# Linear attention on one core: K and V loaded in rows of 8 KB, V's blocks made by masks, the first matmul in 64x64 tiles

## The chip, the cores and the metric

The kernel runs on one core of one Trainium2 chip. The metric is the device time of one execution in microseconds (us), the median of several runs. A profile is taken of one execution; its span runs from the first instruction to the last, and the time measured for a run is a little longer than such a span.

## The reference

Q, K and V are float32 arrays of shape (8, 12, 512, 64): 96 heads, each with 512 rows of 64 numbers.

```
Q_feat = np.maximum(0, Q) + 1
K_feat = np.maximum(0, K) + 1
KV = np.einsum('bhkd,bhkv->bhdv', K_feat, V)
K_sum = np.sum(K_feat, axis=2)
numerator = np.einsum('bhqd,bhdv->bhqv', Q_feat, KV)
denominator = np.einsum('bhqd,bhd->bhq', Q_feat, K_sum)
return numerator / (denominator[:, :, :, None] + 1e-10)
```

Each head needs a 64x64 matrix KV and a vector K_sum of 64 sums, and then every row of Q is multiplied by both.

## The kernel before

**Groups and layout.** The 96 heads are cut into 12 groups of eight heads (NG = 12), and two groups make a pair, so there are six pairs. In SBUF a partition holds whole rows of the sequence. Q is read in "eights": 128 partitions, each with C4 = 32 rows, which is 8 KB of float32 per partition and covers eight heads. K and V are read in "fours": each partition holds C2 = 16 rows, 4 KB of float32, which covers four heads, so that partitions 32b to 32b+31 belong to head b of four. A group is two such fours of K and V.

**Loads.** GpSimd (POOL) issues nearly all transfers, because they cast float32 to bf16 on the way. `load` (line 105) makes a load of K or V: for the first pair one of 512 KB (bf16) per group, later one of 1 MB per pair, which is 2 MB in HBM. `load_q` (line 119) does the same for Q. `load_pair(s)` (line 126) issues K, V and Q of pair s in this order, and each of these three names has two buffers, so the loads of pair s+2 wait on POOL until the groups of pair s have used theirs up. The first Q alone goes over SP's queue and lands as float32 in an output tile (line 93).

**Work on a group g.** `k_features` (line 155) computes max(K + 1, 1) on VectorE (DVE) in two instructions. `v_blocks` (line 162) copies V into v_all: a zeroed buffer in which each partition has four blocks of 64 columns, one for each head of the four, and four more columns with ones; only the block of the partition's own head is filled, so the buffer is a block diagonal. Three of the four copies run on DVE (line 169), the fourth on ScalarE (ACT, line 167); each works on 32 partitions and 2048 elements. `keys_values` (line 180) multiplies: for 16 positions c and two fours n, the 128x64 features are the stationary operand and 260 columns of v_all the moving one, summed in PSUM; n picks the half of PSUM's partitions, and so the column half of TensorE (PE). Block b of the result is KV of head b of the four, and the last four columns are the sums. Four copies on ACT (lines 195 and 196) then bring it into kva, a block-diagonal buffer for two heads. `transposes` (line 198) turns Q's features over (PE, then a copy on ACT, line 209), `out_matmuls` (line 211) multiplies them by kva in 16 matmuls for each half of a pair's heads (h), and `norms` (line 228) divides on DVE: a reciprocal (line 236) and a product (line 237) for each of two PSUM tiles. `output(g)` does this for h = 0 and 1. It needs kva of both groups of its pair. `store` (line 131) issues the result.

**Order.** The order is written by hand and every engine follows it in order. In round g of the loop (line 280) come: the transposes of g-1 if g is odd, k_features(g), v_blocks(g), output(g-2), then either Q's features for the pair (g even) or the transposes of g (g odd), and keys_values(g). At the end of an odd round the loads of a later pair are issued. The stores of groups 0 to 4 are issued in round 7, behind the last loads on POOL's queue; the stores of groups 10 and 11 go over SP's queue, group 11's in five pieces (lines 143 to 148). The last two groups have an order of their own (lines 300 to 315).

**Start.** `clear` (line 251) zeroes a buffer of v_all with a memset on DVE and a copy on ACT, and copies the ones. The identity for the transposes and the zeros of kva are made on POOL.

Of the kernel before, what the change touches and what calls it, by code (L numbers as in the profile page):

```python
# [8 lines left out]
FP32 = mybir.dt.float32  # L9
BF16 = mybir.dt.bfloat16  # L10
ALU = mybir.AluOpType

BANK = 512
# [6 lines left out]
def kernel(  # L20
# [12 lines left out]

    nc = tc.nc  # L40

    B, H, S, D = Q.shape
    P = 128
    C = 8
    C2 = 2 * C
    C4 = 4 * C
# [3 lines left out]
    NG = NPAIR // NP  # L50
    D1 = D + 1
    W = 2 * D1

    def view(t, c):
        return t.flatten_outer_dims().rearrange("(n p c) d -> p n c d", p=P, c=c)

    q_eights = view(Q, C4)
    k_dram = view(K, C2)
    v_dram = view(V, C2)
    o_dram = view(out, C)  # L60

    const = ctx.enter_context(tc.tile_pool(name="const", bufs=1))
    in_pool = ctx.enter_context(tc.tile_pool(name="in_pool", bufs=IN_BUFS))
# [5 lines left out]
    psum_kva = ctx.enter_context(tc.tile_pool(name="psum_kva", bufs=2, space=bass.MemoryType.PSUM))  # L69
# [2 lines left out]

    identity = const.tile([P, P], BF16, name="identity")
    NV = 4
    v_all = const.tile([P, 2, 2, C2, 4 * D1], BF16, name="v_all")
    ones = const.tile([P, 4], BF16, name="ones")
    zero = const.tile([P, 1], FP32, name="zero")
    kva_all = const.tile([P, NV, 4, 2, D1], BF16, name="kva_all")
    kva_diag = [kva_all[:, i] for i in range(NV)]

    drams = dict(k=k_dram, v=v_dram)
    raw = {}
    bufs = {}
# [2 lines left out]
    qts = {}  # L86
    outs = {}
    cells_of = {}

    def load_first_q():  # L90
        t = out_pool.tile([P, 2 * NP, C, D], FP32, name="o_sb")
        half = t[:, 0:NP].rearrange("p n c d -> p (n c) d")
        nc.sync.dma_start(out=half, in_=q_eights[:, 0])
        return half

    def load_rest_q(t):
        u = in_pool.tile([P, 2, C4, D], BF16, name="q_raw")
        nc.gpsimd.dma_start(out=u[:, 1], in_=q_eights[:, 1])
        for e in range(2):
            raw["q", e] = [  # L100
                x.rearrange("p (r c) d -> p r c d", c=C)[:, :, 4 * e : 4 * e + 4]
                for x in (t, u[:, 1])
            ]

    def load(x, groups):
        s = groups[0] // 2
        if groups[0] % 2 == 0 or (x, s) not in bufs:
            bufs[x, s] = in_pool.tile([P, 4, C2, D], BF16, name=f"{x}_raw")
        if len(groups) == 2:
            ms = slice(0, 4)  # L110
            of = slice(4 * s, 4 * s + 4)
        else:
            ms = slice(groups[0] % 2, 4, 2)
            of = slice(4 * s + groups[0] % 2, 4 * s + 4, 2)
        nc.gpsimd.dma_start(out=bufs[x, s][:, ms], in_=drams[x][:, of])  # L115
        for g in groups:
            raw[x, g] = bufs[x, s][:, g % 2 : 4 : 2]

    def load_q(s):
        t = in_pool.tile([P, 2, C4, D], BF16, name="q_raw")  # L120
# [5 lines left out]
    def load_pair(s):  # L126
        load("k", (2 * s, 2 * s + 1))
        load("v", (2 * s, 2 * s + 1))
        load_q(s)
# [25 lines left out]
    def k_features(g):  # L155
        k_raw = raw.pop(("k", g))
        kf = kf_pool.tile([P, C2, 2, D], BF16, name="kf")
        for n in range(2):
            feature(kf[:, :, n], k_raw[:, n])
        kfs[g] = kf  # L160

    def v_blocks(g):
        v_raw = raw.pop(("v", g))
        for b in range(4):
            ps = slice(32 * b, 32 * b + 32)
            if b == 3:
                nc.scalar.copy(out=v_all[ps, g % 2, :, :, b * D : b * D + D], in_=v_raw[ps])  # L167
            else:
                nc.vector.tensor_copy(  # L169
                    out=v_all[ps, g % 2, :, :, b * D : b * D + D], in_=v_raw[ps]  # L170
                )

    def q_features(g):
        q_raw = raw.pop(("q", g))
# [4 lines left out]

    def keys_values(g):  # L180
        kf = kfs.pop(g)
        kva_ps = psum_kva.tile([P, 4 * D1], FP32, name="kva_ps")
        for c in range(C2):
            for n in range(2):
                nc.tensor.matmul(  # L185
                    kva_ps[64 * n : 64 * n + 64],
                    lhsT=kf[:, c, n, :],
                    rhs=v_all[:, g % 2, n, c, :],
                    start=(c == 0),
                    stop=(c == C2 - 1),  # L190
                )
        kva = kva_diag[g % NV]
        for n in range(2):
            ps = slice(64 * n, 64 * n + 64)
            nc.scalar.copy(out=kva[ps, :, n, 0:D], in_=kva_ps[ps, 0 : 4 * D].rearrange("p (b d) -> p b d", b=4))  # L195
            nc.scalar.copy(out=kva[ps, :, n, D], in_=kva_ps[ps, 4 * D : 4 * D1])  # L196

    def transposes(g):
        qf = qfs.pop(g)
        if g % 2 == 0:  # L200
            qts[g // 2] = mid_pool.tile([P, C, P, R], BF16, name="qt")
        for half in range(2):
            qt_ps = psum_qt.tile([P, 2, R, P], BF16, name="qt_ps")
            for c in range(2):
                for r in range(R):
                    nc.tensor.transpose(qt_ps[:, c, r], qf[:, r, 2 * half + c, :, :], identity)  # L206
            copy = nc.vector.tensor_copy if half and g == NG - 2 else nc.scalar.copy
            lo = g % 2 * 4 + 2 * half
            copy(out=qts[g // 2][:, lo : lo + 2], in_=qt_ps.rearrange("p c r q -> p c q r"))  # L209

    def out_matmuls(g, h):
# [3 lines left out]
        for c in range(C):  # L215
            for j in range(2):
                b = 2 * (g % 2) + j
                q = 16 * (4 * h + b)
                nc.tensor.matmul(  # L219
                    ops[c // 4][64 * j : 64 * j + 64, c // 2 % 2, (c % 2) * W : (c % 2) * W + W],  # L220
                    lhsT=qt[:, c, q : q + 16, :],
# [6 lines left out]
    def norms(g, h):  # L228
# [17 lines left out]
    def output(g):  # L246
        for h in range(2):
            out_matmuls(g, h)
            norms(g, h)

    def clear(i):
        t = v_all[:, i].rearrange("p n c x -> p (n c x)").bitcast(FP32)
        w = t.shape[1] * 5 // 8
        nc.vector.memset(t[:, 0:w], 0.0)  # L254
        nc.scalar.copy(out=t[:, w:], in_=zero.to_broadcast([P, t.shape[1] - w]))  # L255
        nc.vector.tensor_copy(
            out=v_all[:, i, :, :, 4 * D : 4 * D1].rearrange("p n c j -> p (n c) j"),
            in_=ones[:, None, :].to_broadcast([P, 2 * C2, 4]),
        )

    with tc.manual_schedule():
        nc.gpsimd.memset(zero, 0.0)
        q_first = load_first_q()
        load("k", (0,))
        load("v", (0,))
        load_rest_q(q_first)
        load("k", (1,))
        load("v", (1,))
        nc.vector.memset(ones, 0.0)
        for b in range(4):  # L270
            nc.vector.memset(ones[32 * b : 32 * b + 32, b : b + 1], 1.0)
        clear(0)
        make_identity(nc, identity)
        for t in kva_diag:
            for b in range(4):
                nc.gpsimd.memset(t[:, b], 0.0)  # L276
        load_pair(1)
        clear(1)
        last = NG - 1
        for g in range(last - 1):  # L280
            if g % 2:
                transposes(g - 1)
            k_features(g)
            v_blocks(g)
            if g >= 2:
                output(g - 2)
            if g % 2:
                transposes(g)
            else:
                q_features(g)  # L290
# [59 lines left out]
```

## Time and profile before

| what | value |
|---|---|
| device time, median of 3 runs | 126.78 us (126.35 to 127.07) |
| span of the profiled execution, the only time it has | 124.5 us |
| last o_sb computed / last store landed | 111.25 us / 123.56 us |
| busy PE, DVE, ACT, POOL | 52%, 72%, 48%, 21% of the span |
| HBM read / written | 37.75 MB / 12.58 MB |
| TensorE clock granted, mean | 0.816 |

In the rows of the profile L185 and the like are lines of the kernel above; times in a timeline count from the span's start. In a row of a group the shape stands as partitions x elements, then the count. The row of slices cuts the span into 40 parts of 3.1 us, each digit the busy share in tenths. PE's row of matmuls and PEld's row of weight loads overlap. A transfer has an issue, on POOL or SP, and lands later; a row of DMA shares above 1.00 means that packets overlap on the 16 engines.

### The profile page before, as it was taken

The page shows a single profiled execution, that of the slowest core. Times are in us where ns is not written, and L with a number is a line of the kernel's source. Part 1 is how long each engine was busy: PE and PEld are TensorE (multiplying, and loading weights), DVE is VectorE, ACT ScalarE, POOL GpSimd, SP SyncE. Part 2 cuts the span into 40 slices and gives each one's busy share as a digit, 9 for nine tenths or more (in the row PEclk, how much of TensorE's full clock was granted, in tenths as well). Part 3 has the DMA queues.
Part 4 walks back from the last instruction along what each step waited for, and adds up shares of the span by engine and source line. Part 5 has one row for each costly group of instructions (what it writes and reads, how often), then busy time and mean ns, then how long its engine had stood idle before and what let it go on. Part 6 is the DMA issues. An engine that isn't in the chain of part 4 may idle for free.

```text
span 124.5 us, 2350 instructions
## 1 busy us (share of the span) xinstructions
PE 65.0 (52%) x960; PEld 53.1 (43%) x960; DVE 89.7 (72%) x190; ACT 59.6 (48%) x86; POOL 26.6 (21%) x53
## 2 busy tenths in 40 slices
PE   0000874600596837939197495987756987420000
PEld 0000754600475736829175374866635766210000
DVE  4875744206999989997999989999599996970000
ACT  7505069706009981398807767169990355000000
POOL 6992020400001310204002194202203302000000
PEclk9999999985559996799859959689985599955555
DMA  3999999999999999999999999999999999999993
GB/s 95 319 211 218 204 209 212 209 215 218 207 212 212 220 215 205 212 213 216 212 213 211 213 219 211 213 209 216 214 295 421 420 419 411 416 414 416 417 407 140
DMA packets 11971, 32.13 MB, mean 258 GB/s; under 512 B 568, under 2 KB 824, under 8 KB 11832
## 3 DMA queue, kind: packets, MB, share of 16 engines
q0 software_dynamic: 10592, 28.84, 97.5%
q1 hardware_dynamic: 1368, 3.15, 6.7%
q8 instruction: 7, 0.11, 0.3%
q14 instruction: 4, 0.03, 0.1%
HBM read 37.75 MB, written 12.58 MB: 404 GB/s over the span
## 4 chain that ended last, share of the span: by engine, by line
DMA 30%; DVE 27%; PE 14%; ACT 10%; POOL 6%; issue 3%; DVEq 0%; ACTq 0%; POOLq 0%
DMA v_raw<-in_V_dram 30%; DVE o_sb L237 12%; PE kva_ps L185 12%; DVE v_all L169 8%; ACT v_all L167 5%; ACT qt L209 3%; DVE recip L236 3%; DVE qf L151 2%; POOL kva_all L276 2%; POOL k_raw L115 2%; ACT kva_all L195 2%; PE qt_ps L206 1%; PE o_ps L219 1%; DVE kf L151 1%; POOL v_raw L115 1%
## 5 line engine op out<-in xcount | busy, mean ns | idle before, releaser
L185 PE MATMUL kva_ps<-v_all,kf 128*64 128x260 bf16 x384 | 34.2, 351 | 15.8 <-DVE v_all L169 14.2
L185 PEld LDWEIGHTS <-kf 128*64 128x64 bf16 x384 | 27.8, 144 | 19.7 <-DVE v_all L169 14.7
L237 DVE TENSOR_TENSOR o_sb<-o_ps,recip 128x512 f32<-128x512 f32 x48 | 33.2, 692 | 1.7
L219 PE MATMUL o_ps<-kva_all,qt 128*64 128x130 bf16 x384 | 19.6, 236 | 28.1 <-DVE recip L236 19.1
L169 DVE COPY v_all<-v_raw 32x2048 bf16<-32x2048 bf16 x36 | 25.5, 710 | 10.5 <-DMA v_raw<-in_V_dram 10.1
L219 PEld LDWEIGHTS <-qt 128*64 128x64 bf16 x384 | 13.7, 116 | 33.1 <-issue 16.9
L167 ACT COPY v_all<-v_raw 32x2048 bf16<-32x2048 bf16 x12 | 22.6, 1894 | 10.8 <-DMA v_raw<-in_V_dram 10.6
L195 ACT CAST kva_all<-kva_ps 64x256 bf16<-64x256 f32 x24 | 8.9, 370 | 31.4 <-PE kva_ps L185 31.2
L209 ACT COPY qt<-qt_ps 128x1024 bf16<-128x1024 bf16 x23 | 22.2, 1015 | 2.5 <-PE qt_ps L206 2.2
L206 PE MATMUL qt_ps<-identity,qf 128*128 128x128 bf16 x192 | 14.1, 229 | 1.3 <-ACT qt L209 1.1
L135 POOL DMA_DIRECT2D out_dram<-o_sb x10 | 8.8, 879 | 23.1 <-DMA q_raw<-in_Q_dram 6.7
L206 PEld LDWEIGHTS <-qf 128*128 128x128 bf16 x192 | 11.8, 103 | 4.1 <-issue 2.2
L115 POOL DMA_DIRECT2D k_raw<-in_K_dram x7 | 5.4, 772 | 37.5 <-DVE kf L151 37.0
L151 DVE TENSOR_SCALAR kf<-k_raw 128x1024 bf16<-128x1024 bf16 x24 | 9.9, 453 | 4.3 <-DMA k_raw<-in_K_dram 4.2
L236 DVE RECIPROCAL recip<-o_ps 128x8 f32<-128x8 f32 x48 | 9.6, 200 | 2.9 <-PE o_ps L219 2.6
L115 POOL DMA_DIRECT2D v_raw<-in_V_dram x7 | 5.4, 768 | 16.5 <-ACT v_all L167 16.5
L151 DVE TENSOR_SCALAR qf<-q_raw 128x1024 bf16<-128x1024 bf16 x22 | 8.1, 424 | 0.0
L254 DVE MEMSET v_all<- 128x2600 f32 x2 | 4.5, 2225 | 1.1 <-issue 1.1
L196 ACT CAST kva_all<-kva_ps 64x4 bf16<-64x4 f32 x24 | 4.1, 169 | 0.0
L121 POOL DMA_DIRECT2D q_raw<-in_Q_dram x5 | 3.5, 704 | 0.0
L255 ACT COPY v_all<-zero 128x1560 f32<-128x1560 f32 x2 | 2.9, 1488 | 0.0
L276 POOL MEMSET kva_all<- 128x130 bf16 x16 | 2.4, 196 | 0.0
(14 smaller groups left out, 6.6 us busy)
## 6 DMA issues: line engine op xcount, KB each, us to landing
out_dram<-o_sb POOLq DMA_DIRECT2D x10, 1024.0 KB, 24.0
k_raw<-in_K_dram POOLq DMA_DIRECT2D x5, 1024.0 KB, 16.7
v_raw<-in_V_dram POOLq DMA_DIRECT2D x5, 1024.0 KB, 17.3
q_raw<-in_Q_dram POOLq DMA_DIRECT2D x5, 1024.0 KB, 21.5
o_sb<-in_Q_dram SPq DMA_DIRECT2D x1, 1024.0 KB, 4.8
k_raw<-in_K_dram POOLq DMA_DIRECT2D x2, 512.0 KB, 9.5
v_raw<-in_V_dram POOLq DMA_DIRECT2D x2, 512.0 KB, 11.3
out_dram<-o_sb SPq DMA_DIRECT2D x1, 1024.0 KB, 12.1
```

Source lines behind the costliest of these rows:

```text
L115: nc.gpsimd.dma_start(out=bufs[x, s][:, ms], in_=drams[x][:, of])
L135: nc.gpsimd.dma_start(out=o_to[:, g % 2 : 2 * NP : 2], in_=outs[s][:, g % 2 : 2 * NP : 2], single_packet=True)
L151: nc.vector.tensor_scalar(out=dst, in0=src, scalar1=1.0, scalar2=1.0, op0=ALU.add, op1=ALU.max)
L167: nc.scalar.copy(out=v_all[ps, g % 2, :, :, b * D : b * D + D], in_=v_raw[ps])
L169: nc.vector.tensor_copy(out=v_all[ps, g % 2, :, :, b * D : b * D + D], in_=v_raw[ps])
L185: nc.tensor.matmul(kva_ps[64 * n : 64 * n + 64], lhsT=kf[:, c, n, :], rhs=v_all[:, g % 2, n, c, :], start=(c == 0), stop=(c == C2 - 1),)
L195: nc.scalar.copy(out=kva[ps, :, n, 0:D], in_=kva_ps[ps, 0 : 4 * D].rearrange("p (b d) -> p b d", b=4))
L206: nc.tensor.transpose(qt_ps[:, c, r], qf[:, r, 2 * half + c, :, :], identity)
L209: copy(out=qts[g // 2][:, lo : lo + 2], in_=qt_ps.rearrange("p c r q -> p c q r"))
L219: nc.tensor.matmul(ops[c // 4][64 * j : 64 * j + 64, c // 2 % 2, (c % 2) * W : (c % 2) * W + W], lhsT=qt[:, c, q : q + 16, :], rhs=kva[:, ...
L236: nc.vector.reciprocal(out=recip, in_=cells[:, :, :, :, D:D1])
L237: nc.vector.tensor_tensor(out=o_sb[:, 2 * h + g % 2 : 2 * NP : NP, 4 * i : 4 * i + 4].rearrange("p n (b c) d -> p b c n d", b=2), in0=cell ...
```

## The change

The fours of K and V become eights, as Q already has them: each partition reads 32 rows, 8 KB of float32 in one piece, and 16 partitions belong to a head. The transfers keep their sizes. In the first pair each group is one eight; later a pair's two eights come in one transfer and a group is one half of the rows (positions) of both eights. So KV of a head is summed over both groups of a pair, and in the first pair over one.

A partition's head is now one of eight: 64 partitions hold four heads, and the two partition halves h hold different heads. `keys_values` therefore multiplies each half by itself: 64 partitions by 64 columns of features, 64 matmuls per group instead of 32, into two PSUM tiles (one for each h), and the copies to kva come once per pair, four of 64x(4x65).

v_all gets four blocks of 68 columns, each with V's 64, a sum column and three of zeros. A mask with one column for each b (made from the identity by a reduction) replaces the copies: each block is V times the mask's column on all 128 partitions. DVE does blocks 0 and 1 and half of block 2, ACT the rest (one instruction of 1024 elements, one of 2048). Nothing has to be cleared but the three zero columns. The line numbers of the functions behind the change shift.

```diff
+    DV = D + 4
-    k_dram = view(K, C2)
-    v_dram = view(V, C2)
+    k_dram = view(K, C4)
+    v_dram = view(V, C4)
...
-    v_all = const.tile([P, 2, 2, C2, 4 * D1], BF16, name="v_all")
-    ones = const.tile([P, 4], BF16, name="ones")
-    zero = const.tile([P, 1], FP32, name="zero")
+    v_all = const.tile([P, 2, 2, C2, 4, DV], BF16, name="v_all")
+    mask = const.tile([P, 4], FP32, name="mask")
...
     def load(x, groups):
         s = groups[0] // 2
-        if groups[0] % 2 == 0 or (x, s) not in bufs:
-            bufs[x, s] = in_pool.tile([P, 4, C2, D], BF16, name=f"{x}_raw")
+        if groups[0] % 2 == 0:
+            bufs[x, s] = in_pool.tile([P, 2, C4, D], BF16, name=f"{x}_raw")
+        t = bufs[x, s]
         if len(groups) == 2:
-            ms = slice(0, 4)
-            of = slice(4 * s, 4 * s + 4)
+            nc.gpsimd.dma_start(out=t, in_=drams[x][:, 2 * s : 2 * s + 2])
         else:
-            ms = slice(groups[0] % 2, 4, 2)
-            of = slice(4 * s + groups[0] % 2, 4 * s + 4, 2)
-        nc.gpsimd.dma_start(out=bufs[x, s][:, ms], in_=drams[x][:, of])
+            n = groups[0] % 2
+            nc.gpsimd.dma_start(out=t[:, n], in_=drams[x][:, 2 * s + n])
         for g in groups:
-            raw[x, g] = bufs[x, s][:, g % 2 : 4 : 2]
+            e = g % 2
+            if s == 0:
+                raw[x, g] = t[:, e].rearrange("p (n c) d -> p n c d", n=2)
+            else:
+                raw[x, g] = t[:, :, C2 * e : C2 * e + C2]
...
     def v_blocks(g):
         v_raw = raw.pop(("v", g))
         for b in range(4):
-            ps = slice(32 * b, 32 * b + 32)
-            if b == 3:
-                nc.scalar.copy(out=v_all[ps, g % 2, :, :, b * D : b * D + D], in_=v_raw[ps])
-            else:
-                nc.vector.tensor_copy(
-                    out=v_all[ps, g % 2, :, :, b * D : b * D + D], in_=v_raw[ps]
-                )
+            block = v_all[:, g % 2, :, :, b, 0:D]
+            cut = 2 if b < 2 else 1 if b == 2 else 0
+            if cut > 0:
+                nc.vector.tensor_scalar_mul(block[:, 0:cut], v_raw[:, 0:cut], mask[:, b : b + 1])
+            if cut < 2:
+                nc.scalar.mul(out=block[:, cut:], in_=v_raw[:, cut:], mul=mask[:, b : b + 1])
...
     def keys_values(g):
         kf = kfs.pop(g)
-        kva_ps = psum_kva.tile([P, 4 * D1], FP32, name="kva_ps")
+        if g % 2 == 0:
+            kva_ps[g // 2] = [psum_kva.tile([P, BANK], FP32, name="kva_ps") for _ in range(2)]
+        halves = kva_ps[g // 2]
         for c in range(C2):
             for n in range(2):
-                nc.tensor.matmul(
-                    kva_ps[64 * n : 64 * n + 64],
-                    lhsT=kf[:, c, n, :],
-                    rhs=v_all[:, g % 2, n, c, :],
-                    start=(c == 0),
-                    stop=(c == C2 - 1),
-                )
-        kva = kva_diag[g % NV]
-        for n in range(2):
-            ps = slice(64 * n, 64 * n + 64)
-            nc.scalar.copy(out=kva[ps, :, n, 0:D], in_=kva_ps[ps, 0 : 4 * D].rearrange("p (b d) -> p b d", b=4))
-            nc.scalar.copy(out=kva[ps, :, n, D], in_=kva_ps[ps, 4 * D : 4 * D1])
+                if g < 2:
+                    eight, first, last_c = g, (c, n) == (0, 0), (c, n) == (C2 - 1, 1)
+                else:
+                    eight, first, last_c = n, g % 2 == 0 and c == 0, g % 2 == 1 and c == C2 - 1
+                for h in range(2):
+                    ps = slice(64 * h, 64 * h + 64)
+                    nc.tensor.matmul(
+                        halves[h][64 * eight : 64 * eight + 64, 0 : 4 * DV],
+                        lhsT=kf[ps, c, n, :],
+                        rhs=v_all[ps, g % 2, n, c],
+                        start=first,
+                        stop=last_c,
+                    )
+        if g % 2 == 0:
+            return
+        for h in range(2):
+            kva = kva_diag[(g - 1 + h) % NV]
+            for n in range(2):
+                ps = slice(64 * n, 64 * n + 64)
+                nc.scalar.copy(
+                    out=kva[ps, :, n, :],
+                    in_=halves[h][ps, 0 : 4 * DV].rearrange("p (b x) -> p b x", b=4)[:, :, 0:D1],
+                )
...
-    def clear(i):
...
+        nc.vector.tensor_reduce(
+            out=mask,
+            in_=identity.rearrange("p (h b x) -> p b h x", h=2, b=4),
+            op=ALU.add,
+            axis=mybir.AxisListType.XY,
+        )
+        for i in range(2):
+            t = v_all[:, i].rearrange("p n c b x -> p (n c) b x")
+            nc.vector.memset(t[:, :, :, D1:], 0.0)
+            nc.vector.tensor_copy(
+                out=t[:, :, :, D], in_=mask[:, None, :].to_broadcast([P, 2 * C2, 4])
+            )
```

More of the change, by code (lines that the diff above doesn't have):

```diff
@@ L88 @@
     cells_of = {}
+    kva_ps = {}
     def load_first_q():
@@ L249, in output @@
             norms(g, h)
-    def clear(i):
[L252 to L258, printed above, removed]
-        )
     with tc.manual_schedule():
-        nc.gpsimd.memset(zero, 0.0)
         q_first = load_first_q()
@@ L268 @@
         load("v", (1,))
[L269 to L272, printed above, removed]
         make_identity(nc, identity)
+        nc.vector.tensor_reduce(
[10 more added lines that the diff above has]
+            )
         for t in kva_diag:
@@ L277 @@
         load_pair(1)
-        clear(1)
         last = NG - 1
```

## The prediction

> **What bounds the kernel now.** I read the slices first, then the queues, then the stretches between landings, then the timelines of ACT and PE for one pair of groups. The slices and the queue, from the page:
>
> ```profile
> DMA  3999999999999999999999999999999999999993
> GB/s 95 319 211 218 204 209 212 209 215 218 207 212 212 220 215 205 212 213 216 212 213 211 213 219 211 213 209 216 214 295 421 420 419 411 416 414 416 417 407 140
> q0 software_dynamic: 10592, 28.84, 97.5%
> ```
>
> From the second slice to the last but one the 16 DMA engines are never idle. Loads count here by their bf16 bytes (212 GB/s written is 424 GB/s read); after 93 us the stores run at 416 GB/s. So the **transfers set the end**: the last o_sb is computed at 111.25, but the last store lands at 123.56 and the span ends at 124.5. Compute may slip until it stands where the transfers end; how far that is, is the question of this change.
>
> The trace marks each landing. Those of pair 1 to 5 follow each other at 4.90, 4.89, 4.94, 4.90, 4.90 us for Q and at 4.95, 4.97, 4.94, 5.01, 5.04, 4.82, 5.00, 4.93 us for K and V, all of 2 MB in HBM. Q has 8 KB rows, K and V have 4 KB rows. The same as stretches, K and V first, then Q (us, busy time of PE, PEld, DVE, ACT, POOL, granted clock, DMA share, GB/s):
>
> ```profile
> 33.97:43.89 9.92, 8.38 (x124) 6.89 (x120) 9.25 (x22) 6.46 (x9) 2.25 (x3) 0.82 1.13 215
> 43.89:48.78 4.89, 2.20 (x46) 1.82 (x44) 4.67 (x10) 2.95 (x6) 0.03 (x1) 0.91 1.05 208
> ```
>
> The longer rows carry no visible advantage in GB/s (the rate counts packets of the neighbouring transfer too); by landings it is 4.906 against 4.958 us. A pair takes 14.75 us of transfers: that is the pace.
>
> ACT over one pair (start, length, line), then PE:
>
> ```profile
> 45.30 1.89 ACT L167 COPY v_all<-v_raw 32x2048 bf16<-32x2048 bf16 x1
> 51.73 0.36 ACT L195 CAST kva_all<-kva_ps 64x256 bf16<-64x256 f32 x1 [4.53 <-PE kva_ps L185]
> 52.65 1.93 ACT L209 COPY qt<-qt_ps 128x1024 bf16<-128x1024 bf16 x2
> 54.60 1.90 ACT L167 COPY v_all<-v_raw 32x2048 bf16<-32x2048 bf16 x1
> 56.60 1.93 ACT L209 COPY qt<-qt_ps 128x1024 bf16<-128x1024 bf16 x2
> 58.96 0.36 ACT L195 CAST kva_all<-kva_ps 64x256 bf16<-64x256 f32 x1 [0.43 <-PE kva_ps L185]
> 59.88 1.89 ACT L167 COPY v_all<-v_raw 32x2048 bf16<-32x2048 bf16 x1
> ```
>
> ```profile
> 48.28 3.40 PE L185 MATMUL kva_ps<-v_all,kf 128*64 128x260 bf16 x32
> 51.62 1.07 PE L206 MATMUL qt_ps<-identity,qf 128*128 128x128 bf16 x16
> 54.85 0.42 PE L219 MATMUL o_ps<-kva_all,qt 128*64 128x130 bf16 x8 [1.59 <-DVE recip L236]
> 56.94 1.98 PE L185 MATMUL kva_ps<-v_all,kf 128*64 128x260 bf16 x32
> ```
>
> These form a **loop** ACT - PE - ACT - PE - ACT: V's blocks of the even group, its keys-values matmuls, its transposes and their copies, V's blocks of the odd group, its matmuls, its casts, and only then, in ACT's order, the next even blocks. Before: 1.9 + 3.4 to 3.7 + 1.08 (four casts) + 1.93 + 1.9 + 2.0 + 1.08 + some 0.35 of hand-overs = 13.8 us. It stands under the pace of 14.75, and ACT's 4.53 us of waiting show the room. DVE needs, per pair, 2x0.75 (kf) + 2x2.05 (L169) + 8x0.845 (L236 with L237) + 1.42 (qf) = 13.8 us, also under it.
>
> **The change, part by part.**
>
> *Rows of 8 KB.* Bytes, number and order of transfers stay; K and V go from 4.958 to Q's 4.906 us. Ten full transfers and four halves: 12 x 0.052 = **-0.6 us**, and only if transfers still set the end. Bounds: 0 (first K, V and Q of 512 KB land 2.48 us apart alike) and -0.7. POOL's issues shorten from 0.77 to Q's 0.70; POOL mostly waits, so this is worth nothing. The Trainium skill (Perfetto Trace Analysis, section DMA Optimizations) says that batching into 4 or 8 KB "can dramatically improve throughput"; by that rule this part would be the gain. The landings above speak against it, since rows of both lengths run side by side here and differ by 1%.
>
> *Start.* Two memsets of 2.23 us and two ACT copies of 1.49 us go; a small reduction behind the identity (POOL, ready near 5.4), two short memsets and copies come. All of it ends near 7.5, before the first K (8.18): nothing. If that cover failed, the first features would start at most 1 us later. But ACT's table load (1.28 us, before at 0.73, long ahead of any data) now stands, in the built order, behind the wait for the first V: V lands at 10.66, the load ends at 12.0.
>
> *V's blocks.* DVE: two products over 2048 and one over 1024 elements for three copies of 2048. By the rows of like shape (copy 0.684, kf 0.42) 1.8 for 2.05 us per group. No row shows a product with a value per partition; bounds are 1.8 and, at the fp32 rows' pace (0.688 per 1024), 3.15. I take 1.8: kf is the same operation with constants. ACT: one over 1024 and one over 2048 for one of 2048. Copy rows give 1.015 + 1.894 = 2.9; I take **3.0**, because the extra operand is in no row; bounds 2.8 and 4.0 (every fixed part twice). The Trainium skill (ScalarE: Activation LUTs, section What ACT_TABLE_LOAD costs) puts 93 ns on each pointer operand: by it 3.1, and the sum 1.2 us later.
>
> *First matmul.* 64 matmuls of 272 columns on four 64x64 tiles for 32 of 260 on two. The row gives a tile one matmul per 0.217 us at half clock (16 in 3.47) and 0.124 at full. If four tiles run side by side: 16 x 0.227 = 3.7 (half clock) or 16 x 0.130 = 2.1, with a tail 2.2 us. If only two do: 7.3 and 4.15. Rows show two column tiles side by side, never two row tiles; I take four, because L219's matmuls follow each other every 0.04 us, so issue leaves room, and keep both ends. In the first pair all of one group goes to one column half, so two tiles work: 32 per tile, half of it before the clock rises, 5.7 us; the second group 4.2.
>
> *Casts.* Eight per pair (4x0.37 and 4x0.17, overlapped: 2.16) become four of 260 columns at 0.37: 1.5, but all after the odd group, so kva of the even group is also late. PSUM for it is one set per pair; it is free, since casts stand ahead of the next even blocks on ACT. Queued behind them: those blocks, and POOL's next V load, which waits for ACT. That load has some 10 us of room (issued 71.1, K ahead of it lands 83.4), of which 6 go.
>
> **The sum.** First pair: 12.0 + 3.0 + 5.7 + 2.5 (transposes 0.55, copies 1.93) + 3.0 + 4.2 + 1.5 + hand-overs = 32.0, where V of pair 1 landed at 29.07; ACT is now late. Loop: 3.0 + 3.7 + 2.5 + 3.0 + 2.2 + 1.5 + 0.35 = **16.25 us**, over the pace. Four of them: casts of group 9 end at 97.0 (before 89.6). From there, as DVE's order is written: four norms of group 8 to 100.9, V blocks and kf of 10 and 11 to 105.3, Q features 106.7, norms of group 9 with its copy 111.3, transposes and matmuls of 11 (start 109.7) 113.0, casts 114.5, eight norms with their start 121.6. Then SP issues the last stores, 0.34 + 0.88 + 0.4 + 0.62 (the store of 5 rows took 4.16 with a full queue ahead; I take the others' 0.4), about 2 us to land (SP's first Q took 4.8, of which 2.5 go to its 1 MB), 0.9 from the last landing to the end of the span: 5.2 in all. Span **126.8** against 124.5. The median shown (126.78) lies 2.3 above the span; so **129.1 us**, 1.8% slower.
>
> **Rivals.**
> 1. *The loop fits* (not slower). If the even matmuls run at full clock (2.2 for 3.7) or ACT is nearer 2.7, the loop is 14.75 to 15.5 and compute ends by 118.7, the point from which the transfers (124.5 - 0.6 = 123.9) set the end again: 126.2 us. For it: the odd matmuls already run at full clock, and L169 gets shorter. Against: PEclk falls to 5 whenever PE is mostly idle, and the even matmuls, at 33.6, 48.3 and 78.4, ran at half; after the change PE waits longer ahead of them. Chance 0.30.
> 2. *Half clock throughout, or tiles that do not overlap by rows*. Odd at half clock too (it was in group 7: 3.42 us): loop 17.75, compute end 129, 136.5 us. No overlap: 5.7 + 4.15 in the loop, 20.2 us, about 149. Chance 0.20, of which 0.07 for no overlap.
> 3. *DVE's product is slow*: 3.15 per group makes DVE's pair 16.0, about the loop's own length, and 2.7 us more in the last groups: 131.8. Chance 0.07.
> 4. *Long rows do lift the rate* (the skill's rule above): at 451 GB/s, the highest window here (3 to 4 us, fp32 without cast), K and V save 3.7 us and the loop must fit as well: 123.1. Chance 0.03.
>
> My forecast has 0.40. **How the numbers follow.** Range: case 1 at 126.0 up to half clock throughout at 136.5, which leaves out no overlap, the worst of 3, and 4. Faster by over 0.5% (what a measurement of this kernel can just tell from no change) needs under 126.15: case 4 and a fifth of case 1, 0.09. Within 0.5% lies most of the rest of case 1: 0.22. Slower: 0.69.
>
> **What would show it.** ACT's blocks at 3.0 per group and its load at 10.7; matmuls of an even group in 3.7 us, of an odd in 2.2; a distance of 16.25 us between the casts of two pairs; slices of DMA below 9 near the end, with gaps; last norm near 121. If the K and V landings stay 4.9 apart and DMA stays at 9 to the last slice, case 1 holds. It is wrong if the matmuls take over 4 us at the end too, or if DVE's products pass 1 us.

## The result, and the profile after

The kernel after takes **128.2 us** (median, 128.08 to 128.22), beside 126.56 (126.13 to 127.07) for the kernel before in the same runs: ratio **1.011, 95% interval 1.007 to 1.015**. The forecast was 129.1 us. The profiled execution has a span of 126.4 us for 124.5. (In later runs some executions of this kernel and its variants were 2 to 4 us longer, most at a lower mean granted clock; the ratios leave them out, all but one of 130.20 us in `rows4k`.)

From the page of the kernel after, the slices and the rows that answer to those of before:

```profile
DMA  3999999999999999999999999999999999999991
GB/s 98 325 216 214 213 213 215 215 213 216 215 211 218 215 210 216 218 213 211 220 209 215 218 211 215 218 211 216 242 407 415 424 407 390 384 380 386 384 313 51
q0 software_dynamic: 7520, 28.84, 93.3%
q8 instruction: 10, 0.16, 0.5%
HBM read 37.75 MB, written 12.58 MB: 398 GB/s over the span
```

The engines of the DMA are as full as before, to the last slice. Loads end earlier: the last one (Q of pair 5) lands at 92.28 for 93.26. But the stores run at 407 to 424 GB/s for four slices, and then at 380 to 390, where the kernel before held 411 to 421. From the last load to the last store it is **33.2 us (92.28 to 125.51), before it was 30.3 (93.26 to 123.56)**, for the same 12.58 MB. A store packet takes 159 to 161 ns (means over 2 us) up to 102 us and 164 to 180 behind it; before, 159 to 163 throughout. The same as stretches of 8 us, kernel before and then kernel after (length, busy time of PE, PEld, DVE, ACT, POOL, granted clock, DMA share, GB/s):

```profile
94.00:102.00 8.00, 6.89 (x79) 5.38 (x80) 7.82 (x17) 2.36 (x6) 1.90 (x2) 0.68 1.03 420
102.00:110.00 8.00, 5.08 (x101) 4.03 (x98) 6.57 (x17) 2.34 (x6) 0.75 (x1) 0.96 1.02 413
110.00:118.00 8.00, 0.27 (x6) 0.02 (x2) 1.21 (x3) 0.00 (x0) 0.00 (x0) 0.50 1.03 417
```

```profile
94.00:102.00 8.00, 4.86 (x91) 3.61 (x94) 7.90 (x18) 5.66 (x4) 0.75 (x1) 0.72 1.03 419
102.00:110.00 8.00, 6.83 (x140) 5.57 (x132) 5.15 (x13) 4.40 (x7) 0.75 (x1) 0.85 1.02 396
110.00:118.00 8.00, 3.64 (x48) 2.30 (x48) 6.33 (x15) 0.03 (x1) 0.00 (x0) 0.58 1.01 377
```

A full share beside fewer GB/s means that each packet takes longer, not that packets are missing: nobody is late in issuing stores.

Compute is later than before, but not as late as forecast. ACT over two pairs of the kernel after (start, length, line; in brackets the idle time ahead), then PE's first matmuls of the same stretch:

```profile
10.54 1.28 ACT L170 ACT_TABLE_LOAD   x1 [10.54 <-DMA v_raw<-in_V_dram]
...
47.61 1.55 ACT L205 CAST kva_all<-kva_ps 64x260 bf16<-64x260 f32 x4 [0.38 <-PE kva_ps L192]
49.18 3.04 ACT L170 ACTIVATE v_all<-v_raw,mask 128x1024 bf16<-128x1024 bf16 x2
54.91 1.93 ACT L221 COPY qt<-qt_ps 128x1024 bf16<-128x1024 bf16 x2 [2.69 <-PE qt_ps L218]
56.72 3.05 ACT L170 ACTIVATE v_all<-v_raw,mask 128x1024 bf16<-128x1024 bf16 x2
...
61.91 1.54 ACT L205 CAST kva_all<-kva_ps 64x260 bf16<-64x260 f32 x4 [0.32 <-PE kva_ps L192]
63.48 3.04 ACT L170 ACTIVATE v_all<-v_raw,mask 128x1024 bf16<-128x1024 bf16 x2
70.82 1.93 ACT L221 COPY qt<-qt_ps 128x1024 bf16<-128x1024 bf16 x2 [4.31 <-PE qt_ps L218]
...
77.82 1.54 ACT L205 CAST kva_all<-kva_ps 64x260 bf16<-64x260 f32 x4 [0.32 <-PE kva_ps L192]
```

```profile
52.27 2.05 PE L192 MATMUL kva_ps<-v_all,kf 64*64 64x272 bf16 x64 [1.15 <-ACT v_all L170]
59.82 2.05 PE L192 MATMUL kva_ps<-v_all,kf 64*64 64x272 bf16 x64 [0.43 <-ACT v_all L170]
66.57 3.60 PE L192 MATMUL kva_ps<-v_all,kf 64*64 64x272 bf16 x64 [1.15 <-ACT v_all L170]
75.73 2.05 PE L192 MATMUL kva_ps<-v_all,kf 64*64 64x272 bf16 x64 [0.87 <-ACT v_all L170]
```

The distance between the casts of two pairs is 14.30 us (47.61 to 61.91) where the even group's 64 matmuls ran at full clock (2.05 us), and 15.91 (61.91 to 77.82) where they ran at half (3.60). The two take turns; the mean of four pairs is 15.1. The last o_sb is computed at 116.57, 5.3 us later than before and 8.9 ahead of the last store. By the prediction's own arithmetic that end of compute would have left the end to the transfers, near 123.9. So the loss stands where no case of the prediction looked: in the stores.

One view misleads here. The page's chain that ended last is led by PE and ACT:

```profile
ACT 37%; PE 34%; DVE 10%; DMA 7%; issue 3%; POOL 1%; ACTq 0%; DVEq 0%; POOLq 0%
```

It follows each step back to what released it. The last stores were released by the last o_sb, so it walks back through compute; that those stores then took 6.1 to 8.6 us from issue to landing, with others still under way, shows only in the issues and landings.

### The profile page after: what moved, and what is told of

Its sections match the earlier page's. It is cut to its first block, busy times and chain, and to the rows that moved or that the text cites. A ratio compares the mean times of both kernels' runs of the same rounds, so it can differ in the third digit from the quotient of the medians.

```text
span 126.4 us, 3095 instructions
## 1 busy us (share of the span) xinstructions
PE 68.5 (54%) x1344; PEld 58.1 (46%) x1344; DVE 82.7 (65%) x186; ACT 67.8 (54%) x72; POOL 24.6 (19%) x52
## 3 DMA queue, kind: packets, MB, share of 16 engines
HBM read 37.75 MB, written 12.58 MB: 398 GB/s over the span
## 4 chain that ended last, share of the span: by engine, by line
ACT 37%; PE 34%; DVE 10%; DMA 7%; issue 3%; POOL 1%; ACTq 0%; DVEq 0%; POOLq 0%
PE kva_ps L192 29%; ACT v_all L170 24%; ACT qt L221 8%; DMA v_raw<-in_V_dram 7%; DVE o_sb L249 7%; ACT kva_all L205 4%; PE qt_ps L218 4%; DVE v_all L168 2%; DVE recip L248 1%; ACT L170 1%; DVE qt L221 1%; PE o_ps L231 1%; POOL k_raw L111 1%; ACTq L353 0%; ACTq L170 0%
## 5 line engine op out<-in xcount | busy, mean ns | idle before, releaser
L192 PE MATMUL kva_ps<-v_all,kf 64*64 64x272 bf16 x768 | 36.6, 324 | 25.9 <-ACT v_all L170 24.4
L192 PEld LDWEIGHTS <-kf 64*64 64x64 bf16 x768 | 33.1, 126 | 27.4 <-DVE v_all L168 14.0
L170 ACT ACTIVATE v_all<-v_raw,mask 128x1024 bf16<-128x1024 bf16 (+1 forms) x24 | 36.4, 1572 | 0.1
L249 DVE TENSOR_TENSOR o_sb<-o_ps,recip 128x512 f32<-128x512 f32 x48 | 33.2, 692 | 1.7
L168 DVE TENSOR_SCALAR v_all<-v_raw,mask 128x2048 bf16<-128x2048 bf16 (+1 forms) x36 | 22.9, 691 | 8.6 <-DMA v_raw<-in_V_dram 8.6
L205 ACT CAST kva_all<-kva_ps 64x260 bf16<-64x260 f32 x24 | 9.0, 374 | 6.2 <-PE kva_ps L192 5.9
L151 DVE TENSOR_SCALAR kf<-k_raw 128x1024 bf16<-128x1024 bf16 x24 | 9.1, 421 | 4.7 <-DMA k_raw<-in_K_dram 4.7
L135 POOL DMA_DIRECT2D out_dram<-o_sb x10 | 7.5, 764 | 23.6 <-DVE o_sb L249 15.0
L108 POOL DMA_DIRECT2D k_raw<-in_K_dram x5 | 3.6, 727 | 32.5 <-DVE kf L151 32.5
L108 POOL DMA_DIRECT2D v_raw<-in_V_dram x5 | 4.0, 792 | 26.7 <-ACT v_all L170 26.7
L280 DVE CAST v_all<-mask 128x128 bf16<-128x128 f32 x2 | 2.2, 1639 | 0.0
## 6 DMA issues: line engine op xcount, KB each, us to landing
k_raw<-in_K_dram POOLq DMA_DIRECT2D x5, 1024.0 KB, 14.3
q_raw<-in_Q_dram POOLq DMA_DIRECT2D x5, 1024.0 KB, 16.5
```

The lines of the kernel that those rows point to most:

```text
L108: nc.gpsimd.dma_start(out=t, in_=drams[x][:, 2 * s : 2 * s + 2])
L135: nc.gpsimd.dma_start(out=o_to[:, g % 2 : 2 * NP : 2], in_=outs[s][:, g % 2 : 2 * NP : 2], single_packet=True)
L151: nc.vector.tensor_scalar(out=dst, in0=src, scalar1=1.0, scalar2=1.0, op0=ALU.add, op1=ALU.max)
L168: nc.vector.tensor_scalar_mul(block[:, 0:cut], v_raw[:, 0:cut], mask[:, b : b + 1])
L170: nc.scalar.mul(out=block[:, cut:], in_=v_raw[:, cut:], mul=mask[:, b : b + 1])
L192: nc.tensor.matmul(halves[h][64 * eight : 64 * eight + 64, 0 : 4 * DV], lhsT=kf[ps, c, n, :], rhs=v_all[ps, g % 2, n, c], start=first, sto ...
```

## The experiments

Three theories stood at the start. **1**: the loop of ACT and PE makes compute late, and that sets the end. **2**: transfers set the end as before, and the slower stores are the price. **Chance**: that one execution had slow stores. All ratios below are to the kernel before.

### Is it there again, and does compute matter?

`again` is the kernel after, unchanged.

> The kernel after, unchanged, to see whether its slow stores come back. In the profiled execution the last load landed at 92.28 us and the last store at 125.51: 33.2 us for the stores, where the kernel before took 30.3 for the same bytes, with store packets of 164 to 180 ns from 102 us on instead of 159 to 163. If this belongs to the change (late compute, or the stores' own order), the packets are as slow again and the time is 128.2. If it was chance, the packets take 160 ns, the stores 30.3 us, and this profile's span is about 92.3 + 30.3 + 0.9 = 123.5.

Median 129.35 us (128.21 to 131.73); ratio 1.012 (1.004 to 1.020). Its profile has a span of 130.0 us and its last load at 97.03, for 126.4 and 92.28, so I compare no end times with it. Its packets take 160 to 164 ns between 96 and 110 us, then 167 to 178: the slow stores are not chance. Its loop is another one than in the first profile, though the program is the same:

```profile
49.28 1.55 ACT L205 CAST kva_all<-kva_ps 64x260 bf16<-64x260 f32 x4 [0.37 <-PE kva_ps L192]
...
65.80 1.55 ACT L205 CAST kva_all<-kva_ps 64x260 bf16<-64x260 f32 x4 [0.32 <-PE kva_ps L192]
```

A pair takes 16.52 us here (49.28 to 65.80), and the even group's matmuls took 3.42 to 3.84 us in all five pairs behind the first. So one and the same program runs its loop in 14.3, 15.9 or 16.5 us, by the clock of the even group.

`early_table` brings ACT's table load ahead of the first V.

```diff
+    warm = const.tile([P, 2], FP32, name="warm")
...
+        nc.vector.memset(warm, 0.0)
+        nc.scalar.copy(out=warm[:, 0:1], in_=warm[:, 1:2])
         make_identity(nc, identity)
```

> ACT's table load is brought ahead of the first V by a copy of one element. Theory 1, the loop of ACT and PE sets the end: the first pair's blocks start 1.3 us earlier and everything behind follows, so the last o_sb ends near 115.3 instead of 116.6 and the time falls by 1.2, to 127.0. Theory 2, the transfers set the end and the stores are slow for a reason of their own: the last o_sb comes earlier by as much and the time stays at 128.2, within 0.3.

128.56 us (128.31 to 128.93), 1.014 (1.009 to 1.020): no gain, as theory 2 said, but for another reason. The first blocks did start earlier (matmuls at 13.7 for 14.9 us). Yet in its profile all even groups ran at half clock, as in that of `again`. ACT and the even group's matmuls of this kernel (its line numbers are one higher):

```profile
64.23 1.55 ACT L206 CAST kva_all<-kva_ps 64x260 bf16<-64x260 f32 x4 [0.32 <-PE kva_ps L193]
65.81 3.04 ACT L171 ACTIVATE v_all<-v_raw,mask 128x1024 bf16<-128x1024 bf16 x2
73.75 1.93 ACT L222 COPY qt<-qt_ps 128x1024 bf16<-128x1024 bf16 x2 [4.90 <-PE qt_ps L219]
...
80.75 1.55 ACT L206 CAST kva_all<-kva_ps 64x260 bf16<-64x260 f32 x4 [0.32 <-PE kva_ps L193]
```

```profile
52.39 3.84 PE L193 MATMUL kva_ps<-v_all,kf 64*64 64x272 bf16 x64 [0.92 <-ACT v_all L171]
```

A pair takes 16.52 us (64.23 to 80.75), close to the forecast's 16.25, and the last o_sb comes at 120.86. The last load comes late as well, at 94.78 for 92.28. POOL issued the last V, which waits for ACT, at 78.91 for 75.98, and V landed 5.70 us behind K for 4.86. The rest of the delay goes with load packets of 580 to 600 ns between 90 and 92 us, where some 330 are usual; why is open. From the last load to the last store (126.24) it is 31.5 us, and a run below with the same tile places needs 31.3. So here too the transfers come last, only later.

**Its store packets took 160 to 162 ns to the end**, though compute ended 4.3 us later than in the profile of the kernel after. So late compute does not slow the packets. What differed? The new tile `warm` moves every tile behind it by 32 bytes.

`block2_dve` makes block 2 of V on DVE alone.

```diff
-            cut = 2 if b < 2 else 1 if b == 2 else 0
+            cut = 2 if b < 3 else 0
```

> Block 2 of V is made on DVE alone, so that ACT keeps one product of 2048 elements per group: ACT 2.0 instead of 3.05 us per group, DVE 2.3 instead of 1.8. Theory 1 (the loop): the loop of a pair falls by 2 x 1.05 from 15.1 to 13.0, under the pace of the loads (14.7), the casts of group 9 come near 89.5 instead of 93.7 and the last o_sb near 112.5; the time falls by 2.5 to 3, to 125.5. Theory 2 (slow stores of their own): compute ends as early, but the store packets stay at 164 to 180 ns and the time is above 127.5.

128.12 us (127.57 to 128.39), 1.011 (1.005 to 1.018). The last o_sb comes at 112.97, 3.6 us earlier than in the kernel after, the last load at 92.38, and the time is the same; packets of 164 to 175 ns from 100 us on. Theory 1 falls for the kernel after: at a loop of 15.1 us compute does not set the end.

`rows4k` cuts the rows of K and V in two again; the first pair's loads and the views of the tiles follow suit.

```diff
-            bufs[x, s] = in_pool.tile([P, 2, C4, D], BF16, name=f"{x}_raw")
+            bufs[x, s] = in_pool.tile([P, 2, 2, C2, D], BF16, name=f"{x}_raw")
...
-            nc.gpsimd.dma_start(out=t, in_=drams[x][:, 2 * s : 2 * s + 2])
+            nc.gpsimd.dma_start(
+                out=t,
+                in_=drams[x][:, 2 * s : 2 * s + 2].rearrange("p n (e c) d -> p e n c d", e=2),
+            )
...
```

> The kernel after with the same transfers of 2 MB for K and V, each row cut in two pieces of 4 KB (the even group's positions and the odd group's); all else is as it was. The loads of K and V should land 4.96 us apart instead of 4.88, and Q's as before: the last load lands 0.5 to 0.8 later, near 93.0. Theory 1 (the loop): the time stays within 0.3 of 128.2, because compute is late in any case. Theory 2 (transfers set the end): 0.6 more, 128.8.

Ratio 1.018 (1.009 to 1.027), executions of 128.43 to 131.71 us: too scattered to tell 0.6 us. The profile shows the part that was asked: last load at 93.04 for 92.28, so the longer rows bring 0.76 us by landings.

### The place of the output tiles

In the built program o_sb begins at byte 140288 of a partition before, at 141792 after: v_all has grown by 1536 bytes, and the mask takes 32 where ones and zero took 64. The first is a multiple of 512, the second lies 32 bytes short of one; with `warm` it is 141824, again a multiple of 512. That is **theory 3**. It needs an edit that moves tiles and nothing else.

```diff
-    mask = const.tile([P, 4], FP32, name="mask")
+    mask = const.tile([P, 16], FP32, name="mask")[:, 0:4]
```

> The kernel after with 48 unused bytes more behind the mask, so that every tile behind it lies 32 bytes further in SBUF. In the kernel after, o_sb, the raw tiles, kf, qf, qt and kva begin at an odd multiple of 32 bytes (o_sb at byte 141792 of a partition), in the kernel before at a multiple of 64 (140288); the run with the early table load, whose store packets stayed at 160 to 162 ns, had shifted them by 32 bytes by accident. Theory 3, the place of the tiles: store packets of 159 to 163 ns to the end, and a store phase (last load to last store) of 30.3 us wherever compute is not later; the time falls below 128.2, to 125.7 if the loop takes 15.1 us a pair as in the profile after, and stays near 128 if it takes 16.5 in this run. Theory 2 without a place (chance, or late stores): packets of 164 to 180 ns from about 9 us after the last load, time 128.2.

```diff
-    zero = const.tile([P, 1], FP32, name="zero")
+    zero = const.tile([P, 16], FP32, name="zero")[:, 0:1]
```

> The kernel before with its tile of zeros 60 bytes longer, so that every tile behind it lies 32 bytes further, o_sb at byte 140320; nothing else changes. Theory 3 (place of the tiles): its stores take 164 to 180 ns a packet from about 9 us after the last load, the store phase 32.5 us for 30.3, and the time rises by 2 us to 128.5, as much as the whole change cost. Theory 2 without a place: 126.5, within 0.3. Theory 1 (the loop) says 126.5 too.

The kernel after with 48 bytes more: **126.52 us, ratio 0.9991 (0.9964 to 1.0017)**. The kernel before with 60 more: **129.14 us (128.96 to 129.67), ratio 1.021 (1.017 to 1.025)**. The loss can be taken from the one and given to the other by the place alone. The stretches of the kernel after with the bytes, then of the kernel before with them:

```profile
94.00:102.00 8.00, 5.19 (x96) 3.77 (x96) 7.90 (x18) 5.32 (x4) 0.75 (x1) 0.70 1.02 417
102.00:110.00 8.00, 6.50 (x136) 5.39 (x128) 5.15 (x12) 4.43 (x7) 0.75 (x1) 0.87 1.03 414
110.00:118.00 8.00, 2.73 (x48) 1.70 (x48) 6.00 (x15) 0.00 (x0) 0.00 (x0) 0.77 1.02 409
```

```profile
94.00:102.00 8.00, 5.18 (x64) 3.94 (x64) 7.83 (x17) 3.00 (x6) 1.84 (x2) 0.79 1.02 418
102.00:110.00 8.00, 5.41 (x100) 4.46 (x102) 6.60 (x16) 2.81 (x6) 0.75 (x1) 0.96 1.02 410
110.00:118.00 8.00, 1.73 (x24) 0.99 (x20) 2.99 (x7) 0.00 (x0) 0.00 (x0) 0.50 1.03 401
```

In the last stretch 409 stands for the kernel after's 377, and 401 for the kernel before's 417. Compute stands near where it stood: last o_sb at 116.23 for 116.57, and at 113.09 for 111.25, 13 us ahead of the last store (126.26). The forecast for the first run, 125.7, was 0.8 too low; the next part comes back to that. The second took 0.6 more than its 128.5; in its profile the loads began later too (last load at 93.82 for 93.26), while the stores took 2.1 us more.

`pad_block2` has the wider mask and block 2 on DVE together.

> Block 2 on DVE alone (compute ends at 113, well before the transfers) and the 48 bytes behind the mask together. Theory 3: last load at 92.4, 30.3 us of stores, 0.9 to the end of the span: span 123.6, time 125.5, faster than the kernel before by 0.6 to 1.0 through its shorter loads. Theory 2 without a place: as the run without the bytes, 128.1.

126.51 us, 0.9983 (0.9958 to 1.0007): 1.6 us less than block 2 on DVE alone, but a microsecond above what was expected. With the place mended, compute that ends at 114.7 or at 116.2 gives the same time.

`pad_out` has the output tiles moved, by the lines below, and block 2 on DVE.

```diff
+    pad_pool = ctx.enter_context(tc.tile_pool(name="pad", bufs=1))
     out_pool = ctx.enter_context(tc.tile_pool(name="out_pool", bufs=OUT_BUFS))
...
+    pad = pad_pool.tile([P, 8], FP32, name="pad")
...
+        nc.vector.memset(pad, 0.0)
```

> Block 2 on DVE alone, with 32 unused bytes in a pool of their own just ahead of the output tiles: only o_sb and the reciprocals move to a multiple of 64 bytes; K, V and Q's tiles, the features and kva stay at odd multiples of 32. If it is the stores' own source that counts, the time is that of the run with all tiles moved, 125.5; if it is where loads land or where the engines write, the packets stay at 164 to 180 ns and the time at 128.1.

126.52 us, 0.9983 (0.9959 to 1.0007), packets of 159 to 162 ns. So it is the **source of the stores** that counts (the reciprocals moved with it, but no transfer reads them). K, V, Q, the features and kva lie at odd multiples of 32 bytes here, and the time and the last load (92.29) are those of `pad_block2`, which moved them too (126.51 and 92.29).

`align64` has a longer pad:

```diff
-    pad = pad_pool.tile([P, 8], FP32, name="pad")
+    pad = pad_pool.tile([P, 24], FP32, name="pad")
```

> The run that moved only the output tiles, with 96 unused bytes instead of 32 ahead of them: o_sb begins at byte 141888 of a partition, a multiple of 64 but not of 128. All places that were fast so far (140288 and 141824) are multiples of 512, those that were slow lie 32 bytes from one. If a multiple of 64 is enough, store packets of 159 to 163 ns and 126.5 us; if a larger one is needed, packets of 164 to 180 ns and 128.1.

127.82 us, 1.009 (1.006 to 1.013), packets of 163 to 179 ns from 102 us on. The last of the three stretches, in the run that moved only the output tiles and then in this one:

```profile
110.00:118.00 8.00, 1.16 (x16) 0.66 (x14) 2.26 (x5) 0.00 (x0) 0.00 (x0) 0.50 1.03 414
```

```profile
110.00:118.00 8.00, 3.60 (x55) 2.17 (x49) 6.54 (x16) 0.28 (x1) 0.00 (x0) 0.65 1.01 377
```

Compute ended later here (last o_sb at 116.81 for 112.33), but 8.4 us ahead of the last store (125.18). A multiple of 64 is not enough; o_sb was fast at multiples of 512 alone, and 128 and 256 were not tried.

The Trainium skill (DMA: Bandwidth & Descriptors, section How a descriptor splits into AXI transactions) says that reads go in pieces of up to 256 bytes that start at a 256-byte boundary, and that bytes ahead of an unaligned start are fetched for nothing. As an estimate from the beats of 32 bytes that the Trainium skill has in that section, a row of 2 KB then costs 65, 66 and 71 beats for 64 in the kernel before with the bytes (32 past a boundary), in this run (64 past) and in the kernel after (224 past): 2, 3 and 11% more. The direction agrees, and that 64 is too little. The sizes don't: beside the run or kernel with the same work in a fast place, the stores took 2.1 us more (32.4 for 30.3), 1.5 (32.9 for 31.4) and 1.9 (33.2 for 31.3), so 7, 5 and 6%. Nor does it say why the first stores, from the same kind of place, ran at 160 ns. That stays open. The traces show one thing about it: the share of store packets above 163 ns lastingly passes a tenth at 101 us in `block2_dve`, at 102 in the kernel after and in this run, at 104 in `rows4k`, at 107 in `again` and at 108 in the kernel before with the bytes. The first fetch of instructions within the stores starts some 2 us or less from there, at 99.7, 103.3, 103.9, 103.5, 109.1 and 107.2 us, in three of the six only afterwards. In the fast places such a fetch leaves the packets at 160 ns, so it isn't the cause by itself; whether it has a part in it was not tried.

### Where the microsecond of the loads went

With the place mended the last load still lands 1.0 us earlier than before (92.23 to 93.26), and the last store at the same time (123.54 to 123.56). The trace marks when each of the 16 engines finished its part of a store. In the kernel before, the last store's marks end with 123.28, 123.31, 123.39, 123.56; in the kernel after with 48 bytes more they end with 122.51, 122.67, **123.51, 123.54**: 14 engines are done 0.9 us earlier, two are not. One of these fell behind at the fifth store (106.12, the next engine 104.92), the other at the eighth (113.61, where the third last is 112.61). The page counts 10 fetches of instructions (q8, 16 KB each) for 7 before, with 2688 matmuls and weight loads on PE for 1920; two of them, 1.04 and 1.03 us long, fall in the stores, at 102.1 and 109.7; before there was one, at 104.3. There one engine finished the fifth store at 106.39, the next at 105.85, but the last store only 0.17 us behind the next. The marks don't name the engine that fetched, so the link is by time alone.

`few_rows` is `pad_out` with this:

```diff
-        for c in range(C2):
+        cs = C2 if g < 7 else C2 // 2 if g == 7 else 4
+        for c in range(cs):
...
-                    eight, first, last_c = n, g % 2 == 0 and c == 0, g % 2 == 1 and c == C2 - 1
+                    eight, first, last_c = n, g % 2 == 0 and c == 0, g % 2 == 1 and c == cs - 1
```

> Only output tiles moved, block 2 on DVE, and fewer PE instructions near the end: the keys-values matmuls leave out half of the positions in group 7 and three quarters in groups 8 to 11 (their KV lacks these), 2242 instructions on PE for 2690. With the whole work two fetches of 16 KB of instructions fall between the last load and the last store, each holds one DMA engine for 1.0 us, and two engines finish 0.9 to 1.2 us behind the other 14, at 123.6. If these fetches eat the microsecond that the loads of 8 KB rows gain, the fetches in the stores go, all 16 engines finish by 122.7, and the time falls by 0.9 to 125.6. If the late engines have another cause, they are late again and the time stays at 126.5. Compute is earlier too, but it already ended at 112.3, 11 us ahead of the last store.

**125.67 us, 0.9946 (0.9908 to 0.9983)**, 0.85 less than with all matmuls by the medians, 0.6 by the means; the two intervals overlap. In its profile one fetch, at 99.9, still falls in the stores; the marks end with 122.92, 123.11, 123.22, 123.40, with no engine apart. That execution's loads ended late (93.13), but its stores took 30.3 us where `pad_out` took 31.4. This agrees with the fetches, in size too. It doesn't isolate them: PE had less to do as well, though the last o_sb came no earlier (112.56 for 112.33).

`pad_rows4k` joins the edits of `rows4k` and `pad_out`.

> Only output tiles moved, block 2 on DVE, and K and V's rows in two pieces of 4 KB: what the longer rows are worth where stores are not slowed. Last load near 93.0 for 92.3. If transfers set the end, 0.5 to 0.8 more than the same kernel with 8 KB rows: 127.1. If the gain of the loads is lost behind them in any case, 126.5.

126.95 us (1.002, 0.999 to 1.005) beside 126.52: 0.43 us by the medians, 0.57 by the means; here too the intervals overlap. The last load lands at 93.24 for 92.29, the span is 125.2 for 124.6. The rows of 8 KB are worth about half a microsecond.

### When compute does set the end

`act_heavy` is the kernel after with the wider mask and this:

```diff
-            cut = 2 if b < 2 else 1 if b == 2 else 0
+            cut = 2 if b < 2 else 0
```

> All tiles at a multiple of 64 bytes, and block 2 of V wholly on ACT: 4.0 us per group for 3.05, so that the loop of a pair is 1.9 us longer, 17.0 for 15.1 as in the profile after. Theory 1 in its limits (compute sets the end once its last o_sb comes after 118.7): last o_sb near 125, span 130.3, time 132.3. If even this loop does not set the end, 126.5 as without it.

139.34 us, 1.10 (1.09 to 1.11), 7 more than expected. The DMA slices of its page, then casts from ACT's timeline:

```profile
DMA  3999999999999999999649999599999999987392
```

```profile
53.27 1.55 ACT L205 CAST kva_all<-kva_ps 64x260 bf16<-64x260 f32 x4 [2.04 <-PE kva_ps L192]
...
71.40 1.55 ACT L205 CAST kva_all<-kva_ps 64x260 bf16<-64x260 f32 x4 [0.32 <-PE kva_ps L192]
```

Here the gaps that theory 1 asks for are there: DMA slices of 4 to 6 among the loads and one of 3 near the end, last o_sb at 132.04, 5.6 us to the end of the span. The loop is 18.1 to 19.4 us, not 17.0: with 0.85 us more on ACT in each group, all even groups ran at half clock (3.3 to 3.8 us) and some odd ones too (3.7). The step was mis-sized because the clock was taken as given.

## Why the prediction was right and wrong

- **The time, 129.1 for 128.2**, and the sign were right by luck; the path to them was not. The span came out at 126.4 for 126.8 because two errors met: compute ended 5.0 us earlier than forecast, and the stores took 2.9 us more than before's 30.3, 1.9 of it by the place of their source. The other 0.5 us lies in the step from span to time, 2.3 in the forecast and 1.8 in the profiled execution (128.2 for 126.4).
- **The step that failed** is the end of the sum, "compute end 121.6", which then set the end of the span. Measured, 116.57. It is made of: first pair 1.3 us later (the second group's matmuls took 5.33 for 4.2), four loops of 15.1 for 16.25 (4.6 less), the last groups 22.9 for 24.6 (1.7 less). The loop's parts were right: ACT's blocks 3.04, casts 1.54, odd matmuls 2.05, even ones 3.60 at half clock. But they ran at half clock in every second pair only, where the sum had it in all. The profile that has them at half clock in all four (the early table load) shows 16.52 us, 120.86 and a span of 127.16, near the forecast's 16.25, 121.6 and 126.8. Even there compute is not shown to set the end: the last load came 2.5 us later, which the forecast had ruled out by V's 10 us of room, and the stores took their 31.5 us from there. What decides the clock of an even group stays open. It isn't PE's wait just ahead, which was 1.15 us both before the matmuls of 2.05 us at 52.27 and before those of 3.60 at 66.57.
- **Rival 1 was the right mechanism**: even matmuls at full clock, loop 14.3 in those pairs, compute done before 118.7, transfers set the end. It gave 126.2; with the output tiles in a good place the kernel takes 126.5. (Its other condition, ACT at 2.7, makes a loop of 15.65 us, not 15.5.)
- **The term that was missing**: "Bytes, number and order of transfers stay" was true and not enough. The place of the stores' source changed, worth 1.7 us (128.2 to 126.52). The built program's tile addresses were there to be read before the run.
- **Rows of 8 KB**: forecast -0.6 (0 to -0.7) if transfers set the end; measured 0.76 to 0.95 by the last load, 0.43 in the time. Rival 4, the rule of the Trainium skill (Perfetto Trace Analysis, section DMA Optimizations), is out: the loads of pairs 2 to 5 took 58.8 us for 59.3. (That section of the Trainium skill speaks of small transfers made larger; here the transfers stayed at 2 MB and only the rows grew.) Before, that is 14.82 us a pair, not 14.75.
- **Table load**: at 10.54, behind V's landing, as forecast. But taking it away did not help: 128.56 with it early, 126.52 with the same tile places and it late. In the profile with it early the even matmuls ran at half clock and the last load came late. That the earlier start did this is not shown, since `again` has the same without it; for it speaks that the four executions of `early_table` had mean clocks of 0.807 to 0.846, the first four of the kernel after 0.861 to 0.885.
- **V's blocks**: DVE 1.9 per group (22.9 us in 12) for 1.8, so rival 3 is out. ACT 3.04 per group for 3.0. The Trainium skill (ScalarE: Activation LUTs, section What ACT_TABLE_LOAD costs) had 3.1 with its 93 ns per pointer operand; the 2048 took 1.99 for a copy's 1.89, which agrees with it.
- **64x64 tiles**: four side by side, 2.05 and 3.6 us for 64, against 2.1 to 2.2 and 3.7. No overlap by rows is out.
- **What would show it**: loads at 4.9 us and DMA at 9 to the last slices were named as the sign of case 1, and that is what the page showed.

## What to carry to other kernels

When a kernel ends in its stores, write down where the stores' source tiles begin before and after an edit: any tile allocated ahead of them moves them, and here 32 bytes cost 1.3 to 2%. Full DMA slices with fewer GB/s mean slower packets; look at the packet's time and at the place of its source before blaming whoever issues late. And a loop whose matmuls may run at either clock has two lengths: give both, and don't take one profile's for the kernel's.

## What the runs showed that I had not expected

- Stores from o_sb at bytes 141792, 141888 and 140320 of a partition fell from 418 or 419 GB/s (94 to 102 us) to 377, 377 and 401 (110 to 118 us); from 140288 and 141824, multiples of 512, they held 409 to 417.
- The same program can have its even groups at half clock in every second pair (3.60 and 2.05 us in turn) or in all (3.42 to 3.84 us, `again`). The Trainium skill (TensorE: Matmul & The Clock Gate, section Part 1: The HAM clock gate) says that the window by which the clock is set runs freely and does not start with the kernel; that one start of the program gave turns of 14.30 and 15.91 us and another 16.52 throughout agrees with it, but no run here varies the window alone.
- A fetch of 16 KB of instructions takes 0.9 to 1.0 us in the stores, and in the kernel after with 48 bytes more one engine's part of every later store is late by about as much, from 106.12 for 104.92 to 123.54 for 122.67 at the end. That this is the engine that fetched is inferred from the time.
